# A 3x3 convolution in bf16: the first block's rows load ahead of the weights, and the fifth image pair loads in 8 and 56 rows

## The chip, the core and the metric

The kernel runs on one core of a Trainium2 chip. The metric is device time in microseconds of one execution. The core has five engines with an instruction stream each: TensorE (PE; its weight loads are listed as PEld), VectorE (DVE), ScalarE (ACT), GpSimd (POOL) and SyncE (SP). SyncE and GpSimd issue the DMAs of this kernel, each on a queue of its own (SyncE's is q1, GpSimd's q0), and 16 DMA engines carry them out.

## The reference

A 3x3 convolution with zero padding of 1, over 16 images of 64 channels of 64x64, to 128 output channels. The weights are 90% zeros, which the kernel does not use.

```python
batch, c_in, h, w, c_out, k = 16, 64, 64, 64, 128, 3
x_pad = np.pad(x, ((0, 0), (0, 0), (pad, pad), (pad, pad)))
output[b, co] += weight[co, ci, kh, kw] * x_pad[b, ci, kh:kh+h, kw:kw+w]   # over ci, kh, kw
```

In memory that is 16.8 MB of input, 0.3 MB of weights and 33.6 MB of output, all float32.

## The kernel before, in words

**Tiling.** The 16 images form 8 pairs: the 64 channels of two images fill the 128 partitions. Each pair's 64 rows are 4 blocks of 16 output rows, so there are 32 blocks, `k` from 0 to 31. A block is computed two rows at a time, in the manner of a fast convolution along the rows: with input rows a, b, c, d (a the odd row above, b and c the pair itself, d below), TensorE makes three products per block:

- `ps[0]`: (b + c) times the middle kernel row, G1. The sums b + c are the tile `sums`, made by `fill_sums`.
- `ps[1]`: odd rows (a and c) times G0 and G21 = G2 - G1. The odd rows are the tile `odd`, made by `fill_odd`.
- `ps[2]` or `ps[3]`: even rows (b and d) times G01 = G0 - G1 and G2. The even rows are the tile `even`, made by `fill_even`.

That is 6, 12 and 12 matmuls, 30 per block, half of them for each of the two images. ScalarE copies `ps[0]` to `pc` (L276); VectorE adds `pc` to `ps[1]` and to the last product and writes the even and odd output rows (L289, L293).

**Loads.** Pairs are loaded in bf16 by GpSimd's casting DMAs (`load`, L101 to 103), in the pieces that `PIECES` gives. Only the first 32 rows of pair 0 (`HEAD`) come in float32 by SyncE, into `x_head` (L98), behind the weights (L95). GpSimd issues the rest of pair 0 and pairs 1 to 3 at once; the pieces of pairs 4 to 7 are issued behind the blocks that `WHEN` names (L44, L269): pair 4's first piece behind block 1's fills, its second behind block 6's, and so on. Pair 4 comes in rows 0 to 28 and 28 to 64 (L41).

**Weights.** VectorE and ScalarE cast the 128x576 weights to bf16 in six pieces (L198). TensorE transposes them, three matmuls for each kernel row (L241), ScalarE copies G1 and G2 out of PSUM (L228, L230), VectorE copies G0 (L215) and makes the two differences G21 and G01 (L212). TensorE runs matmuls on a tile of zeros, `keep_busy`, ahead of the transposes and behind them, seven and seven (L237).

**Fills of block 0.** VectorE makes the sums between its two differences and the even rows behind them; ScalarE makes the odd rows behind its last weight copy. From block 1 on, GpSimd makes sums and even rows and ScalarE the odd rows, always one block or more ahead.

**Order of TensorE.** It waits for all four of ScalarE's weight steps, sets `s_free` to 1 itself, and enters a loop over two blocks at a time. In each block it takes `s_odd` and `s_sum`, makes the first product, takes `s_free`, makes the second, takes `s_even`, and makes the third.

**Stores.** SyncE stores a pair's 4.2 MB when its four blocks are done (L306), the last two pairs in halves, and the last half behind the section (L355). The four output buffers are used in turn; the fourth one, `home`, lies over `x_head` and the inputs of pairs 0 to 2.

Of the kernel before, what the change touches and what calls it, by code (L numbers as in the profile page):

```python
# [13 lines left out]
G0, G1, G2, G21, G01 = range(5)  # L14
# [8 lines left out]
def kernel(  # L23
# [6 lines left out]
    nc = tc.nc  # L30
    B, C_IN, H, W = x.shape
    C_OUT, _, KH, KW = weight.shape
    assert (B, C_IN, H, W) == (16, 64, 64, 64) and (C_OUT, KH, KW) == (128, 3, 3)
    NP = B // 2
    HEAD = 32
    N = NP * BLOCKS
    HALVED = (6, 7)

    PIECES = {p: [(0, H)] for p in range(NP)}
    PIECES[0] = [(HEAD, H)]  # L40
    PIECES[4] = [(0, 28), (28, H)]  # L41
    for p in (5, 6, 7):
        PIECES[p] = [(0, H // 2), (H // 2, H)]
    WHEN = {1: (4, 0), 6: (4, 1), 8: (5, 0), 11: (5, 1), 14: (6, 0), 17: (6, 1), 20: (7, 0), 24: (7, 1)}  # L44
# [4 lines left out]
    def sem(name):  # L49
        return nc.alloc_semaphore(name)  # L50

    def pair(p):
        return x[2 * p : 2 * p + 2].rearrange("n i h w -> (n i) h w")
# [4 lines left out]
    x_head = home[:, 0, :].rearrange("c (h w) -> c h w", w=W)  # L58
# [18 lines left out]
    pc = [sbuf(f"pc{k}", [128, 2, HALF, W], FP32) for k in range(3)]  # L77
    ps = [nc.alloc_psum_tensor(f"ps{k}", [128, 2, HALF, W], FP32).ap() for k in range(4)]

    s_w, s_head = sem("s_w"), sem("s_head")  # L80
    s_x = [[sem(f"s_x{p}{i}") for i in range(len(PIECES[p]))] for p in range(NP)]
    s_st = [[sem(f"s_st{p}{h}") for h in range(2 if p in HALVED else 1)] for p in range(NP)]
    s_dve, s_act, s_id, s_tr = sem("s_dve"), sem("s_act"), sem("s_id"), sem("s_tr")
    s_sum, s_even = ([sem(f"s_{n}{k}") for k in range(UNROLL)] for n in ("sum", "even"))
    s_odd, s_free = sem("s_odd"), sem("s_free")
    s_pe, s_pc, s_out, s_late = sem("s_pe"), sem("s_pc"), sem("s_out"), sem("s_late")

    def into(p, a, b):
        return out[2 * p : 2 * p + 2].rearrange("n o h w -> o n h w")[:, :, a:b, :]
# [2 lines left out]
    section.__enter__()  # L92


    nc.sync.dma_start(out=w_sb, in_=weight.rearrange("o i kh kw -> o (i kh kw)")).then_inc(  # L95
        s_w, 16
    )
    nc.sync.dma_start(out=x_head, in_=pair(0)[:, 0:HEAD, :]).then_inc(s_head, 16)  # L98


    def load(p, i=0):  # L101
        a, b = PIECES[p][i]
        nc.gpsimd.dma_start(out=xs[p][:, a:b, :], in_=pair(p)[:, a:b, :]).then_inc(s_x[p][i], 16)  # L103
# [5 lines left out]
        out=ident,  # L109
        in_=ident,  # L110
# [8 lines left out]
    def source(p, r):  # L119
        if r < 0 or r >= H:  # L120
            return None, None
        if p == 0 and r < HEAD:
            return x_head, (s_head, 16)
        return xs[p], (next(s for (a, b), s in zip(PIECES[p], s_x[p]) if r < b), 16)

    def rows_of(k, first, count):

        p = k // BLOCKS
        pieces = []
        for i, r in enumerate(range(first, first + 2 * count, 2)):  # L130
            src, landed = source(p, r)
            if pieces and pieces[-1][2] is src:
                pieces[-1][1] += 1
                pieces[-1][4].append(landed)
            else:
                pieces.append([i, 1, src, r, [landed]])
        return sorted(pieces, key=lambda q: q[2] is not None)
# [3 lines left out]
    def wait(engine, s, value):  # L141
        key = (engine.engine, s.name)
        if waited.get(key, 0) < value:
            engine.wait_ge(s, value)  # L144
            waited[key] = value

    def fill(engine, copy, zero, tile_, k, first, count, done):
        for i, c, src, r, landed in rows_of(k, first, count):
            if src is None:
                last = zero(tile_[:, i, :])  # L150
            else:
                for s in landed:
                    wait(engine, *s)
                last = copy(tile_[:, i : i + c, :], src[:, r : r + 2 * c - 1 : 2, :])
        last.then_inc(done, 1)

    def fill_odd(k, engine=None, copy=None, zero=None, done=None):
        r0 = ROWS * (k % BLOCKS)
        fill(
            engine or nc.scalar,  # L160
            copy or (lambda o, i: nc.scalar.copy(out=o, in_=i)),  # L161
            zero or (lambda o: nc.scalar.copy(out=o, in_=zeros)),
            odd[k % UNROLL], k, r0 - 1, HALF + 1, done or s_odd,
        )

    def fill_even(k, engine=None, copy=None, zero=None, done=None):
        r0 = ROWS * (k % BLOCKS)
        fill(
            engine or nc.gpsimd,
            copy or (lambda o, i: nc.gpsimd.tensor_copy(out=o, in_=i)),  # L170
            zero or (lambda o: nc.gpsimd.memset(o, 0.0)),  # L171
            even[k % UNROLL], k, r0, HALF + 1, done or s_even[k % UNROLL],
        )

    def fill_sums(k, engine=nc.gpsimd):
        p, b = divmod(k, BLOCKS)
        r0 = ROWS * b
        src = source(p, r0)[0]
        for r in (r0, r0 + ROWS - 1):
            wait(engine, *source(p, r)[1])  # L180
        engine.tensor_tensor(  # L181
            out=sums[k % UNROLL],
            in0=src[:, r0 : r0 + ROWS : 2, :],
            in1=src[:, r0 + 1 : r0 + ROWS : 2, :],
            op=ADD,
        ).then_inc(s_sum[k % UNROLL], 1)
# [6 lines left out]
    wps = {g: v.rearrange("o (j c) -> o j c", c=128) for g, v in  # L193
           ((G1, flat[2][:, 0, :]), (G0, flat[2][:, 1, :]), (G2, flat[3][:, 1, :]))}

    def cast(g, copy, a, b, done):
        k = 3 * g + a % 3
        copy(out=w_bf4[:, g, a:b, :], in_=w_v[:, k : k + b - a, :]).then_inc(done, 1)  # L198


    v = nc.vector
    v.memset(idle_rhs, 0.0).then_inc(s_dve, 1)  # L202
    v.wait_ge(s_w, 16)
    cast(G1, v.tensor_copy, 0, 3, s_dve)
    cast(G0, v.tensor_copy, 0, 3, s_dve)
    cast(G0, v.tensor_copy, 3, 4, s_dve)
    cast(G2, v.tensor_copy, 3, 4, s_dve)
    vcopy = lambda o, i: v.tensor_copy(out=o, in_=i)
    vzero = lambda o: v.memset(o, 0.0)

    def difference(g, wps):
        return v.tensor_tensor(out=wT[:, g], in0=wps[:, 0:3, :], in1=wT[:, G1], op=SUB)  # L212

    v.wait_ge(s_tr, 2)
    v.tensor_copy(out=wT[:, G0], in_=wps[G0][:, 0:3, :])  # L215
    v.wait_ge(s_act, 4)
    difference(G21, wps[G2])
    fill_sums(0, v)
    difference(G01, wps[G0])
    fill_even(0, v, vcopy, vzero)  # L220


    a = nc.scalar
    a.wait_ge(s_w, 16)
    cast(G1, a.copy, 3, 4, s_act)
    cast(G2, a.copy, 0, 3, s_act)
# [6 lines left out]
    t = nc.tensor  # L233

    def keep_busy(n):
        for _ in range(n):
            t.matmul(idle_ps, idle_rhs[:, 0:128], idle_rhs, start=True, stop=True)  # L237

    def transposed(g):
        for j in range(3):  # L240
            mm = t.matmul(  # L241
                wps[g][:, j, :], w_bf[:, g, C_IN * j : C_IN * (j + 2)], ident,
                start=True, stop=True,
            )
        mm.then_inc(s_tr, 1)

    t.wait_ge(s_dve, 1)
    keep_busy(7)
    t.wait_ge(s_id, 2)
    t.wait_ge(s_act, 1)  # L250
    t.wait_ge(s_dve, 2)
# [3 lines left out]
    t.wait_ge(s_dve, 5)  # L255
    t.wait_ge(s_act, 2)
    transposed(G2)
    keep_busy(7)


    g = nc.gpsimd
    for p in (1, 2, 3):
        load(p)
    for k in range(1, N):
        for fill_in, product in ((fill_sums, 2), (fill_even, 6)):
            if k >= UNROLL:
                wait(g, s_pe, 6 * (k - UNROLL) + product)
            fill_in(k)
        if k in WHEN:  # L269
            load(*WHEN[k])  # L270


    fill_odd(0)
    for k in range(N):
        wait(a, s_pe, 6 * k + 2)
        a.copy(out=pc[k % 3], in_=ps[0]).then_inc(s_pc, 1)  # L276
# [4 lines left out]
    for k in range(N):  # L281
        p, b = divmod(k, BLOCKS)
        o = outs[p % 4]
        r0 = ROWS * b
        if p >= 4:
# [4 lines left out]
            out=o[:, :, r0 : r0 + ROWS : 2, :], in0=ps[1], in1=pc[k % 3], op=ADD  # L290
# [3 lines left out]
            out=o[:, :, r0 + 1 : r0 + ROWS : 2, :], in0=ps[2 + k % 2], in1=pc[k % 3], op=ADD  # L294
# [4 lines left out]
    for p in range(NP):  # L299
        parts = 2 if p in HALVED else 1  # L300
        rows = H // parts
        for h in range(parts):
            if (p, h) == (NP - 1, 1):
# [3 lines left out]
                out=into(p, rows * h, rows * (h + 1)),  # L307
                in_=outs[p % 4][:, :, rows * h : rows * (h + 1), :],
# [22 lines left out]
    def take(s):  # L331
        t.wait_ge(s, 1).then_inc(s, -1)  # L332

    t.wait_ge(s_act, 4)
    t.sem_inc(s_free, 1)
    turn = t.alloc_register("turn")
    t.reg_mov(turn, 0)
    nc.br("blocks", engines=[PE])
# [15 lines left out]
    with tc.manual_schedule():  # L354
        nc.sync.dma_start(  # L355
            out=into(NP - 1, H // 2, H), in_=outs[(NP - 1) % 4][:, :, H // 2 : H, :]
# [36 lines left out]
```

## Time and profile before

| | |
|---|---|
| runs | 126.42 us, median of 3 (125.88 to 127.98) |
| profiled execution | 126.62 us, of which the span of its instructions is 124.8 us |
| busy share of the span | PE 88%, DVE 66%, POOL 52%, PEld 45%, ACT 44% |
| mean granted TensorE clock over the span | 0.963 (1.00 in every stretch until 115 us) |
| share of the DMA engines' time | q1 (SyncE) 66.9%, q0 (GpSimd) 31.0% |
| memory traffic | 17.07 MB read, 33.55 MB written, 406 GB/s over the span |
| SyncE's issues | weights 0.95, head 1.40, first store 22.73, last store 113.76 us |
| landing behind the issue | weights 2.8, head 5.9, pair 0's other half 8.0, pair 4's two pieces 17.1 and 13.4, last store 10.2 us |
| TensorE's first and last block | from 8.28, to 110.92 us |

A profile lists instructions by the line that issued them and by the tile that they write and read. Idle time of an engine is shown with what ended it. All times run from the first instruction of the span. The GB/s of a casting load count the bytes that it writes, in bf16; it reads twice as many.

### The profile page before, as it was taken

What the parts mean: (1) busy time and instruction counts of PE and PEld (TensorE: products, weight loads), DVE (VectorE), ACT (ScalarE), POOL (GpSimd) and SP (SyncE); (2) the same over time, 40 slices, a digit from 0 to 9 for tenths busy, and PEclk for the clock granted to TensorE, in tenths of its full rate; (3) what the DMA queues carried; (4) which work ended last, traced back from release to release, by engine and by line L of the source; (5) the groups of instructions that cost most, each with busy time, mean ns of one, the idle gap of its engine ahead of it and who ended that gap; (6) DMA issues with size and microseconds to landing.
All of it is one profiled execution on the core that took longest, in us unless ns stands there. A gap on an engine that the chain in (4) does not pass through costs nothing.

```text
span 124.8 us, 2486 instructions
## 1 busy us (share of the span) xinstructions
PE 110.0 (88%) x983; PEld 56.5 (45%) x983; DVE 82.6 (66%) x74; ACT 54.5 (44%) x78; POOL 64.3 (52%) x89
## 2 busy tenths in 40 slices
PE   5979999999999999999999999999999999990000
PEld 1435555555555555555555555555555555540000
DVE  0576777777777777777777777777777777773000
ACT  4524555555555555554444444444444555530000
POOL 4469555575755755755675575557555555100000
PEclk9999999999999999999999999999999999999555
DMA  3999999999999999999999999999999999999990
GB/s 109 350 219 221 215 218 213 191 429 407 342 330 285 390 410 356 338 427 349 374 370 345 364 432 345 341 416 420 352 339 428 431 407 428 423 428 428 426 391 32
DMA packets 4739, 42.79 MB, mean 343 GB/s; under 512 B 384, under 2 KB 384, under 8 KB 1664
## 3 DMA queue, kind: packets, MB, share of 16 engines
q1 hardware_dynamic: 3008, 34.90, 66.9%
q0 software_dynamic: 1728, 7.87, 31.0%
q14 instruction: 3, 0.02, 0.0%
HBM read 17.07 MB, written 33.55 MB: 406 GB/s over the span
## 4 chain that ended last, share of the span: by engine, by line
PE 82%; DVE 2%; issue 0%; DVEq 0%
PE ps L321 82%; DVE home L293 1%; DVE home L289 1%; DVEq L144 0%
## 5 line engine op out<-in xcount | busy, mean ns | idle before, releaser
L276 ACT COPY pc<-ps 128x1024 f32<-128x1024 f32 x32 | 32.4, 1012 | 51.9 <-PE ps L321 51.9
L321 PE MATMUL ps<-odd,wT 64*128 64x504 bf16 (+1 forms) x384 | 47.2, 377 | 0.0
L321 PE MATMUL ps<-even,wT 64*128 64x504 bf16 (+1 forms) x384 | 47.2, 377 | 0.0
L289 DVE TENSOR_TENSOR o<-ps,pc 128x1024 f32<-128x1024 f32 x24 | 29.4, 1225 | 19.6 <-PE ps L321 19.6
L321 PEld LDWEIGHTS ps<-even,wT 64*128 64x128 bf16 x384 | 21.6, 94 | 19.9
L321 PEld LDWEIGHTS ps<-odd,wT 64*128 64x128 bf16 x384 | 21.6, 94 | 19.9
L293 DVE TENSOR_TENSOR o<-ps,pc 128x1024 f32<-128x1024 f32 x24 | 29.4, 1225 | 0.0
L321 PE MATMUL ps<-sums,wT 64*128 64x504 bf16 (+1 forms) x192 | 26.5, 377 | 0.7 <-PEq L332 0.7
L181 POOL TENSOR_TENSOR sums<-x 128x512 bf16<-128x512 bf16 x20 | 23.1, 1154 | 0.1
L170 POOL COPY even<-x 128x576 bf16<-128x576 bf16 (+1 forms) x20 | 13.0, 650 | 19.2 <-PE ps L321 19.2
L321 PEld LDWEIGHTS ps<-sums,wT 64*128 64x128 bf16 x192 | 10.7, 94 | 10.9 <-issue 1.2
L181 POOL TENSOR_TENSOR sums<-home 128x512 bf16<-128x512 bf16 (+1 forms) x11 | 13.3, 1212 | 2.8 <-DMA home<-in_x_dram 2.8
L289 DVE TENSOR_TENSOR home<-ps,pc 128x1024 f32<-128x1024 f32 x8 | 9.8, 1225 | 6.3 <-PE ps L321 6.3
L161 ACT COPY odd<-x 128x576 bf16<-128x576 bf16 (+1 forms) x20 | 13.2, 660 | 0.0
L170 POOL COPY even<-home 128x576 bf16<-128x576 bf16 (+2 forms) x11 | 6.7, 609 | 8.2 <-PE ps L321 8.0
L293 DVE TENSOR_TENSOR home<-ps,pc 128x1024 f32<-128x1024 f32 x8 | 9.8, 1225 | 0.0
L161 ACT COPY odd<-home 128x576 bf16<-128x576 bf16 (+1 forms) x10 | 6.6, 657 | 0.0
L171 POOL MEMSET even<- 128x64 bf16 x8 | 1.2, 151 | 10.3 <-PE ps L321 10.3
L237 PE MATMUL ps<-idle_rhs 128*128 128x512 bf16 x14 | 5.3, 538 | 1.4 <-DVE idle_rhs L202 1.4
L103 POOL DMA_DIRECT2D x<-in_x_dram x9 | 5.1, 565 | 0.0
L237 PEld LDWEIGHTS ps<-idle_rhs 128*128 128x128 bf16 x14 | 1.7, 129 | 3.7 <-issue 1.9
L198 DVE CAST w_bf<-w_sb 128x192 bf16<-128x192 f32 (+1 forms) x4 | 1.1, 352 | 2.4 <-DMA w_sb<-in_weight_dram 2.4
(21 smaller groups left out, 15.2 us busy)
## 6 DMA issues: line engine op xcount, KB each, us to landing
out_dram<-o SPq DMA_DIRECT2D x5, 4096.0 KB, 18.4
out_dram<-home SPq DMA_DIRECT2D x1, 4096.0 KB, 19.1
out_dram<-o SPq DMA_DIRECT2D x2, 2048.0 KB, 14.4
out_dram<-home SPq DMA_DIRECT2D x2, 2048.0 KB, 11.1
x<-in_x_dram POOLq DMA_DIRECT2D x6, 512.0 KB, 13.1
home<-in_x_dram POOLq DMA_DIRECT2D x2, 1024.0 KB, 13.5
home<-in_x_dram SPq DMA_DIRECT2D x1, 1024.0 KB, 5.9
x<-in_x_dram POOLq DMA_DIRECT2D x1, 1024.0 KB, 20.0
```

Of the source, the lines that this page charges most:

```text
L103: nc.gpsimd.dma_start(out=xs[p][:, a:b, :], in_=pair(p)[:, a:b, :]).then_inc(s_x[p][i], 16)
L161: copy or (lambda o, i: nc.scalar.copy(out=o, in_=i)),
L170: copy or (lambda o, i: nc.gpsimd.tensor_copy(out=o, in_=i)),
L171: zero or (lambda o: nc.gpsimd.memset(o, 0.0)),
L181: engine.tensor_tensor(out=sums[k % UNROLL], in0=src[:, r0 : r0 + ROWS : 2, :], in1=src[:, r0 + 1 : r0 + ROWS : 2, :], op=ADD,).then_inc(s ...
L198: copy(out=w_bf4[:, g, a:b, :], in_=w_v[:, k : k + b - a, :]).then_inc(done, 1)
L237: t.matmul(idle_ps, idle_rhs[:, 0:128], idle_rhs, start=True, stop=True)
L276: a.copy(out=pc[k % 3], in_=ps[0]).then_inc(s_pc, 1)
L289: v.tensor_tensor(out=o[:, :, r0 : r0 + ROWS : 2, :], in0=ps[1], in1=pc[k % 3], op=ADD).then_inc(s_free, 1)
L293: v.tensor_tensor(out=o[:, :, r0 + 1 : r0 + ROWS : 2, :], in0=ps[2 + k % 2], in1=pc[k % 3], op=ADD).then_inc(s_out, 1)
L321: mm = t.matmul(into[:, n, :, c_lo:c_hi], tap(g, kw, n), src[q, i : i + HALF, c_lo + kw - 1 : c_hi + kw - 1], start=(m == 0), stop=(m == l ...
```

## The change

The head load is cut in two: 17 rows ahead of the weights, 15 behind them, with a semaphore each. Block 0 needs input rows 0 to 16 alone. Its three fills now stand ahead of the weights' steps: the sums first on VectorE, the odd rows first on ScalarE (behind the clear of the zeros tile), the even rows on GpSimd (behind its loads) instead of VectorE. TensorE waits for three of ScalarE's steps instead of four; VectorE releases the second product with its first difference (`s_free`), and the third with its second difference, for which it waits until GpSimd's even rows are done (`s_first`). The fillers are nine ahead of the transposes and three behind them, instead of seven and seven. Pair 4 is loaded as rows 0 to 8 and 8 to 64; the times at which its two pieces are issued stay.

```diff
-    HEAD = 32
+    HEAD, FIRST = 32, 17
...
-    PIECES[4] = [(0, 28), (28, H)]
+    PIECES[4] = [(0, 8), (8, H)]
...
-    s_w, s_head = sem("s_w"), sem("s_head")
+    s_w, s_head = sem("s_w"), [sem(f"s_head{i}") for i in range(2)]
...
-    s_odd, s_free = sem("s_odd"), sem("s_free")
+    s_odd, s_free, s_first = sem("s_odd"), sem("s_free"), sem("s_first")
...
+    def load_head(i, a, b):
+        nc.sync.dma_start(out=x_head[:, a:b, :], in_=pair(0)[:, a:b, :]).then_inc(s_head[i], 16)
+
+    load_head(0, 0, FIRST)
     nc.sync.dma_start(out=w_sb, in_=weight.rearrange("o i kh kw -> o (i kh kw)")).then_inc(
         s_w, 16
     )
-    nc.sync.dma_start(out=x_head, in_=pair(0)[:, 0:HEAD, :]).then_inc(s_head, 16)
+    load_head(1, FIRST, HEAD)
...
         if p == 0 and r < HEAD:
-            return x_head, (s_head, 16)
+            return x_head, (s_head[0 if r < FIRST else 1], 16)
...
     v.memset(idle_rhs, 0.0).then_inc(s_dve, 1)
+    fill_sums(0, v)
     v.wait_ge(s_w, 16)
...
     v.wait_ge(s_act, 4)
-    difference(G21, wps[G2])
-    fill_sums(0, v)
-    difference(G01, wps[G0])
-    fill_even(0, v, vcopy, vzero)
+    difference(G21, wps[G2]).then_inc(s_free, 1)
+    v.wait_ge(s_first, 1)
+    difference(G01, wps[G0]).then_inc(s_even[0], 1)
...
     a = nc.scalar
+    a.wait_ge(s_dve, 1)
+    fill_odd(0)
     a.wait_ge(s_w, 16)
...
-    keep_busy(7)
+    keep_busy(9)
...
     transposed(G2)
-    keep_busy(7)
+    keep_busy(3)
...
     for p in (1, 2, 3):
         load(p)
+    fill_even(0, done=s_first)
...
-    fill_odd(0)
     for k in range(N):
         wait(a, s_pe, 6 * k + 2)
...
-    t.wait_ge(s_act, 4)
-    t.sem_inc(s_free, 1)
+    t.wait_ge(s_act, 3)
```

More of the change, by code (lines that the diff above doesn't have):

```diff
@@ L207 @@
     cast(G2, v.tensor_copy, 3, 4, s_dve)
-    vcopy = lambda o, i: v.tensor_copy(out=o, in_=i)
-    vzero = lambda o: v.memset(o, 0.0)
     def difference(g, wps):
```

## Prediction

> **What bounds the kernel now.** I read the page first, then the chain of waits that ended last, then stretches of the span with their DMA share, then the timeline of SyncE's issues, and last the timeline of the first ten microseconds, where the change sits. The page's head, its DMA slices and its HBM line:
>
> ```profile
> span 124.8 us, 2486 instructions
> ...
> DMA  3999999999999999999999999999999999999990
> ...
> HBM read 17.07 MB, written 33.55 MB: 406 GB/s over the span
> ```
>
> The chain that ended last:
>
> ```profile
> 8.28 102.64 PE ps L321 x948
> ...
> 112.24 1.23 DVE home L293
> ```
>
> The two seem to disagree. The chain says: TensorE runs from 8.28 us without a hole to 110.92, VectorE finishes, and whatever starts TensorE sooner ends the kernel sooner. The DMA row says that the 16 DMA engines are full from the second slice to the last but one. The stretches decide (columns: stretch, its length, busy time of PE, PEld, DVE, ACT, POOL, the granted TensorE clock, DMA share, GB/s moved):
>
> ```profile
> 1.00:2.00 1.00, 0.60 (x2) 0.28 (x3) 0.27 (x1) 1.00 (x1) 0.55 (x1) 1.00 0.05 12
> 2.00:3.00 1.00, 1.00 (x4) 0.30 (x2) 0.00 (x0) 0.19 (x1) 0.65 (x3) 1.00 0.97 261
> 3.00:8.00 5.00, 4.54 (x20) 1.88 (x18) 2.90 (x8) 2.46 (x6) 2.20 (x4) 1.00 1.04 307
> 8.00:22.00 14.00, 13.72 (x128) 7.23 (x130) 10.28 (x11) 6.51 (x10) 9.56 (x13) 1.00 1.05 218
> ...
> 24.00:25.00 1.00, 1.00 (x13) 0.53 (x10) 1.00 (x2) 0.00 (x0) 0.26 (x1) 1.00 1.01 176
> 25.00:26.00 1.00, 1.00 (x13) 0.48 (x11) 0.94 (x1) 0.64 (x1) 0.98 (x3) 1.00 1.24 456
> ...
> 97.00:101.00 4.00, 4.00 (x41) 2.04 (x37) 2.71 (x3) 2.43 (x5) 2.57 (x3) 1.00 1.02 438
> 105.00:113.80 8.80, 7.19 (x68) 3.49 (x62) 6.88 (x6) 2.60 (x3) 0.70 (x2) 1.00 1.01 428
> 113.80:121.00 7.20, 0.00 (x0) 0.00 (x0) 0.00 (x0) 0.00 (x0) 0.00 (x0) 0.62 1.01 428
> 121.00:122.00 1.00, 0.00 (x0) 0.00 (x0) 0.00 (x0) 0.00 (x0) 0.00 (x0) 0.50 0.45 188
> 122.00:123.00 1.00, 0.00 (x0) 0.00 (x0) 0.00 (x0) 0.00 (x0) 0.00 (x0) 0.50 0.12 49
> ```
>
> From 2.0 us to 121 us the DMA share is about 1.0 in every stretch: loads alone until 25, loads and stores mixed, stores alone at 428. (A casting load counts its bf16 bytes, so 218 is 436 read.) The end confirms it. After 113.8 us the queues still move 7.2 us at 428 GB/s plus about 0.24 MB, 3.3 MB in all, while the last store, issued at 113.76, holds 2.1 MB. So 1.2 MB, 2.8 us of work, lay ahead of it. **The kernel is bound by the DMA engines, not by TensorE**: 17.07 MB read and 33.55 MB written pass in 119 us, and TensorE has slack at its end. The last row also shows that some engines finish up to 2 us after most: the span ends with the slowest of the 16.
>
> **What the change touches, from the timeline of the start:**
>
> ```profile
> 3.74 1.15 DVE L198 CAST w_bf<-w_sb 128x192 bf16<-128x192 f32 x4 [2.40 <-DMA w_sb<-in_weight_dram]
> ...
> 5.44 2.10 PE L237 MATMUL ps<-idle_rhs 128*128 128x512 bf16 x7
> ...
> 7.37 0.69 DVE L181 TENSOR_TENSOR sums<-home 128x512 bf16<-128x512 f32 x1 [0.62 <-DMA home<-in_x_dram]
> ...
> 8.28 0.82 PE L321 MATMUL ps<-sums,wT 64*128 64x512 bf16 x6 [0.74 <-PEq L332]
> ```
>
> Today the weights are seen at 3.74; the 32 head rows at 7.37, and the sums that VectorE makes from them let block 0 go at 8.28.
>
> **Head split, 17 rows ahead of the weights.** SyncE issues three DMAs instead of two (0.39 and 0.42 us each, from 0.95): 0.95, 1.40, 1.82. First bytes come at 2.0, as now, and a request issued at 1.82 is in time for a queue that is full beyond 4, so no hole opens. The 17 rows are 17 x 256 B x 128 = 557 KB; at the 350 to 390 GB/s seen between 3 and 6 us that is 1.5 us (1.3 at 428, 1.8 at the 307 of 3 to 8). The rows are seen at about 4.1 (2.0 + 1.5, and the 0.6 that the weights' landing shows behind their last bytes), the weights at 3.74 + 1.5 = 5.24 instead of 3.74. The last 15 rows land with the same bytes before them as the 32 did, 7.4 plus nothing I can see. The price of cutting a transfer: rows of 16 KB go at 438 GB/s (97 to 101 us), rows of 8 KB at 428 (105 to 113.8), so halving a row costs at most 2.3%, 0.06 us on 1.05 MB.
>
> **Work moved into the wait for the weights.** Sums (0.692 us, VectorE) run at 4.1 to 4.8, odd rows (0.247 + 0.617 us, ScalarE; the zero row right behind the table load, which ends at 2.19) end at 4.75, both before 5.24. Even rows go from VectorE (0.741) to GpSimd (0.603 for 128x512, so some 0.68 for 128x576): GpSimd has issued its loads by 4.66, so 4.7 to 5.4, inside its 2.77 us wait, ahead of the sums of block 1, which wait for the last 15 rows (7.42 now). All of it costs nothing while the weights are the later of the two. If the 17 rows came after the weights' turn instead, ScalarE's 0.62 would stand ahead of its weight casts and the chain below would slip by up to 0.6.
>
> **Weights to block 0.** Today's transposes run from 4.38 and the filler behind them from 5.44, 1.70 after the weights are seen. Three fillers instead of seven are 3 x 0.30 = 0.90 us. So block 0 can go at 5.24 + 1.70 + 0.90 = 7.84, or 8.1 if the last transpose's modelled end (5.64) counts: **8.0, 0.3 us earlier** than 8.28 (7.7 to 8.6 with the ends of the head's rate). The wait on TensorE is now for three of ScalarE's steps, not four; the first difference releases the odd product: 6.75 - 3.74 = 3.0 behind the weights, 8.25, and that product is due at 8.0 + 0.64 = 8.64. The second follows at 8.8, due at 9.94; behind it on VectorE waits only the first output sum, due at 10.2. Without these margins of 0.4 and 1.1 us TensorE would wait for VectorE. The seven-to-nine fillers ahead of the weights fill a longer wait.
>
> **Fifth pair in 8 and 56 rows.** Queued before the first store there are now 20 rows fewer: 655 KB read, 1.5 us at 436. The load queue, which hands over to stores at 25.0, runs out at 23.5. The first store is issued 14.45 us behind block 0's start (22.73 - 8.28): 22.45 now. The SyncE request of 0.95 moves bytes from 2.0, so a store into an empty queue starts about 1.05 behind its issue: 23.5. The hand-over is just closed, 0 expected. The 56 rows, issued at about 25.1, carry 655 KB more and land later: the 36 rows land at 25.35 + 13.4 = 38.8 now, 3 us more at half the engines is 41.8. GpSimd first needs them for block 16's sums at 54.6. A row of 1 KB after the cast may be slow: the weights' 2.3 KB rows ran at 261 GB/s in their second, so 262 KB cost between 0.6 and 1.0 us; I take +0.1 of that 0.4.
>
> The Trainium skill, page "DMA: Bandwidth & Descriptors", section "Anatomy of one DMA", speaks against cutting transfers: each DMA has a fixed cost of about 2.0 us beside bytes over 436 GB/s. By it the one DMA more could make the sum 126.5 + 2.0 = 128.5. The trace sides with hiding: the stretch 105 to 113.8 holds the join between two stores and shows a share of 1.01.
>
> **The sum**, against the profiled execution's own 126.62 us (span 124.8, 1.8 outside it): bytes unchanged, first byte unchanged, +0.06 for the head, +0.1 for the short rows, 0 for the hand-over (0 to +0.6 if block 0 goes at 8.6), 0 for TensorE's 0.3 since it has slack. 126.8. That execution lies 0.2 above the median of the three runs, so for the median: 126.42 + 0.15, **126.5 us**.
>
> **Rivals.**
> *The end follows TensorE* (chance 0.13). The chain says so. Then the gain is what block 0 gains, 0.3, at most 0.6: 126.1. Against: 1.2 MB queued ahead of the last store. A gain of 2% is out of reach even so: block 0 would have to start at 5.8, 0.5 us after the weights are there.
> *The weights come late, and the load-to-store hand-over opens* (0.10, slower). If the weights were served with all of the head, they would be seen at 7.4, block 0 would go at 7.4 + 2.75 = 10.2, the first store at 24.6, its bytes at 25.7, against loads that end at 23.5: 2.2 us of empty engines. It decides from a block 0 later than 8.0, one for one. The engines that finish early have up to 2 us to give; the last one reads some 1.5 us longer, so between 0.5 and 2.2 is paid: 127.9. For: loads from GpSimd are in the queues as well. Against: SyncE's head, issued at 1.40, landed in 5.9 us and GpSimd's half pair, issued at 1.45, in 8.0, so what SyncE asks is not held up by it; and the weights are issued ahead of the rest.
> A rule of the Trainium skill, same page, section "Queues, rings and completion order", that engines go round robin between queues, would support this rival; the two landings do not show it here at the start.
> *A bubble per DMA* (0.05). One more request with a hole of its own: the weights' 288 KB took 2.8 us to land, 2.1 more than 0.7 of transfer: 128.6. The Trainium skill's fixed cost per DMA, cited above, would act like this.
> *The 56 rows are late* (0.02): only if they land 13 us later than worked out; a stall of 3 us would give 129.5.
>
> **How the numbers follow.** Forecast 0.70: 126.5, own range 126.0 to 127.2, as runs of the kernel before lie at 125.88 to 127.98 and the slowest engine moves the end by some tenths. The range 125.6 to 127.8 takes in the first rival and most of the second. A measurement here can tell about 2% (2.5 us) from no change. Faster by that has no mechanism but an evener finish of the DMA engines (2 us at most): 0.03. Slower: the late rows, and the upper ends of hand-over and bubble: 0.07. Within: 0.90.
>
> **What would show it.** In the changed kernel's profile: weights seen near 5.2, sums near 4.1, block 0 near 8.0, DMA share 1.0 in every stretch from 2 to 121 and no dip between 23 and 26, the last store landing about 10.5 us behind its issue (10.2 now, plus what TensorE gained). A wrong forecast would show as a stretch with a share under 0.9 before 121, or an end that moves with block 0.

## The result, and the profile after

The changed kernel takes 129.09 us (median of 6 runs, 128.90 to 129.23) against 125.99 for the kernel before (125.75 to 127.98): a ratio of 1.0244, 95% interval 1.0223 to 1.0266 (the ratio leaves out the one slow execution, 127.98). It is **slower by 3.1 us**; the forecast was 126.5, and the range ended at 127.8. The profiled execution took 129.23 us, span 127.4, which is 2.6 more than the span before; the profile before is of an execution of 126.62, 0.6 above its median, so the profiles differ by less than the medians. The page's head, DMA row and HBM line:

```profile
span 127.4 us, 2482 instructions
...
DMA  3999999699999999999999999999999999999991
...
HBM read 17.07 MB, written 33.55 MB: 397 GB/s over the span
```

The bytes are the same. The DMA row now has a 6 in its eighth slice, near 24 us, where it had a 9. The stretches of the changed kernel (columns as before: stretch, length, PE, PEld, DVE, ACT, POOL, clock, DMA share, GB/s):

```profile
2.00:4.00 2.00, 2.00 (x7) 0.67 (x5) 0.00 (x0) 0.43 (x2) 1.62 (x5) 1.00 0.83 228
...
8.00:10.00 2.00, 2.00 (x10) 0.53 (x9) 1.46 (x3) 0.48 (x1) 0.00 (x0) 0.58 1.14 288
10.00:12.00 2.00, 2.00 (x14) 0.75 (x12) 0.00 (x0) 1.14 (x2) 0.08 (x1) 0.57 1.01 218
...
24.00:25.00 1.00, 1.00 (x14) 0.46 (x10) 0.65 (x1) 0.93 (x2) 1.00 (x2) 1.00 0.39 62
25.00:25.60 0.60, 0.60 (x10) 0.24 (x8) 0.16 (x1) 0.60 (x2) 0.27 (x1) 1.00 0.07 27
...
26.00:30.00 4.00, 4.00 (x40) 1.84 (x38) 3.20 (x4) 1.58 (x2) 2.40 (x4) 1.00 1.00 418
...
115.70:124.00 8.30, 0.00 (x0) 0.00 (x0) 0.00 (x0) 0.00 (x0) 0.00 (x0) 0.61 1.01 426
```

Three things are new: a slow start (228 GB/s from 2 to 4 us), a TensorE clock of 0.57 to 0.58 from 8 to 12 us, and DMA engines that are more than half empty from 24 to 25 and nearly empty from 25 to 25.6 (shares of 0.39 and 0.07). The end is as before: after the last store's issue the engines are full at 426. The start, for comparison, in the kernel before:

```profile
2.00:4.00 2.00, 2.00 (x7) 0.60 (x4) 0.26 (x1) 0.45 (x3) 1.62 (x5) 1.00 1.08 326
```

The timeline of the changed kernel (start, duration, engine, line), in two excerpts, the second of TensorE and SyncE alone:

```profile
1.87 0.42 SPq L96 DMA_DIRECT2D home<-in_x_dram  x1
...
5.50 0.69 DVE L185 TENSOR_TENSOR sums<-home 128x512 bf16<-128x512 f32 x1 [4.15 <-DMA home<-in_x_dram]
...
6.41 1.15 DVE L202 CAST w_bf<-w_sb 128x192 bf16<-128x192 f32 x4 [0.23 <-DMA w_sb<-in_weight_dram]
...
7.05 0.95 PE L245 MATMUL ps<-ident,w_bf 128*128 128x128 bf16 x9 [1.83 <-DVE w_bf L202]
...
11.92 1.27 POOL L185 TENSOR_TENSOR sums<-home 128x512 bf16<-128x512 f32 x1 [5.21 <-DMA home<-in_x_dram]
```

```profile
8.79 1.46 PE L325 MATMUL ps<-sums,wT 64*128 64x512 bf16 x6
...
13.47 0.81 PE L325 MATMUL ps<-sums,wT 64*128 64x512 bf16 x6
```

```profile
24.68 26.31 SPq L310 DMA_DIRECT2D out_dram<-o  x3
```

The 17 rows are seen at 5.50 (4.1 was forecast), the weights at 6.41 (5.24), block 0 goes at 8.79 (8.0). The last 15 rows, issued at 1.87, are seen only at 11.92 (7.4 was forecast): GpSimd waits 5.2 us for them. Block 1 starts 4.7 us behind block 0 instead of 3.24 (13.47 behind 8.79; in the kernel before 11.52, below, behind 8.28), and the first store is issued at 24.68 instead of 22.73.

```profile
11.52 0.83 PE L321 MATMUL ps<-sums,wT 64*128 64x512 bf16 x6
```

**Why the last 15 rows are late.** The DMA queues from 7 to 10 us, the kernel before first, then the changed one (packets, MB, share of 16 engines):

```profile
q0 software_dynamic: 129, 0.66, 107.1%
q1 hardware_dynamic: 1, 0.00, 0.0%
```

```profile
q0 software_dynamic: 102, 0.49, 78.8%
q1 hardware_dynamic: 99, 0.36, 31.2%
```

Before, SyncE's 32 rows shared the engines with GpSimd's loads from 4 to 7 us (98 packets of q1, 63 of q0) and were through at 7. Now SyncE has a third request behind the other two, and its 15 rows (q1) still share the engines with the loads from 7 to 10, packet by packet: 99 packets against 102. The Trainium skill, page "DMA: Bandwidth & Descriptors", section "Queues, rings and completion order", says that an engine goes round robin between its queues; this trace agrees (99 against 102), and the 15 rows of 3.8 KB were paired with loads that read 8 and 16 KB. Part of the lateness is the slow start: in e9 below, where the loads come a little later, the rows are seen at 9.9, still not at 7.4.

**Where the rest of the time went.** From 30 to 34 us, first before, then after:

```profile
q1 hardware_dynamic: 73, 1.20, 71.3%
q0 software_dynamic: 62, 0.29, 34.9%
```

```profile
q1 hardware_dynamic: 73, 1.20, 93.8%
q0 software_dynamic: 12, 0.09, 10.3%
```

The same 73 store packets took 71.3% of the engines' 4 us in one kernel and 93.8% in the other: 0.62 and 0.82 us each. The share is full both times, the bytes are not: with the loads counted by what they read (twice their MB) 1.20 + 0.58 = 1.78 MB before, 1.38 MB after. **A full DMA share is not a full rate.** The stretch lies just ahead of where the load queue, which ran dry at 25, comes back with the 56 rows: the first of them move at 33, and from 31 to 33 the stores, alone in the engines, took 1.0 us each (110.0% of 32 us, 16 engines times 2 us, over 35 packets):

```profile
q1 hardware_dynamic: 35, 0.57, 110.0%
```

Against the kernel before, the changed one lost in bytes, at the 428 GB/s of the end: 0.20 MB from 2 to 4 us (0.5 us), 0.47 MB from 24 to 26 (0.85 against 0.38; 1.1 us), 0.40 MB from 30 to 34 (0.9 us). That is 2.5 us; smaller stretches bring it to 2.9 by 42 us (table below), against 2.6 us more of span, so the account closes to some 0.3 us.

### The profile page after: what moved, and what is told of

Same layout as the page of the kernel before. It is cut to its first block, busy times and chain, and to the rows that moved or that the text cites. A ratio compares the mean times of both kernels' runs of the same rounds, so it can differ in the third digit from the quotient of the medians.

```text
span 127.4 us, 2482 instructions
## 1 busy us (share of the span) xinstructions
PE 110.8 (87%) x981; PEld 48.7 (38%) x981; DVE 82.0 (64%) x73; ACT 54.8 (43%) x78; POOL 64.8 (51%) x90
## 4 chain that ended last, share of the span: by engine, by line
PE 83%; DMA 4%; DVE 3%; SPq 0%; issue 0%; DVEq 0%
PE ps L325 82%; DMA w_sb<-in_weight_dram 4%; DVE home L297 1%; DVE home L293 1%; DVE w_bf L202 1%; PE ps L241 1%; PE ps L245 0%; SPq L96 0%; SPq L391 0%; DVEq L148 0%; SPq L92 0%
## 5 line engine op out<-in xcount | busy, mean ns | idle before, releaser
L325 PE MATMUL ps<-even,wT 64*128 64x504 bf16 (+1 forms) x384 | 46.7, 377 | 0.0
L325 PEld LDWEIGHTS ps<-odd,wT 64*128 64x128 bf16 x384 | 18.9, 96 | 23.8 <-issue 1.6
L325 PEld LDWEIGHTS ps<-even,wT 64*128 64x128 bf16 x384 | 18.6, 94 | 22.9
L325 PEld LDWEIGHTS ps<-sums,wT 64*128 64x128 bf16 x192 | 9.3, 95 | 12.0 <-issue 1.1
L241 PE MATMUL ps<-idle_rhs 128*128 128x512 bf16 x12 | 4.8, 569 | 1.4 <-DVE idle_rhs L206 1.4
L185 DVE TENSOR_TENSOR sums<-home 128x512 bf16<-128x512 f32 x1 | 0.7, 691 | 4.2 <-DMA home<-in_x_dram 4.2
L165 ACT CAST odd<-home 128x512 bf16<-128x512 f32 (+2 forms) x3 | 1.5, 512 | 3.6 <-DMA home<-in_x_dram 3.6
## 6 DMA issues: line engine op xcount, KB each, us to landing
x<-in_x_dram POOLq DMA_DIRECT2D x1, 896.0 KB, 14.5
```

The source lines that it names most:

```text
L185: engine.tensor_tensor(out=sums[k % UNROLL], in0=src[:, r0 : r0 + ROWS : 2, :], in1=src[:, r0 + 1 : r0 + ROWS : 2, :], op=ADD,).then_inc(s ...
L325: mm = t.matmul(into[:, n, :, c_lo:c_hi], tap(g, kw, n), src[q, i : i + HALF, c_lo + kw - 1 : c_hi + kw - 1], start=(m == 0), stop=(m == l ...
```

## The experiments

For all kernels the table gives what the profiled execution shows: when block 0 starts, when the first store is issued, the MB moved between 2 and 42 us (q1 plus twice q0, of the DMA view of that stretch), how far that falls short of the kernel before, in us at 428 GB/s, and by how much that same execution is above 125.95 us, the median of the kernel before; then the median and the ratio of the timed comparison.

| kernel | block 0 | first store | MB, 2 to 42 | short, us | above, us | median us | ratio (95%) |
|---|---|---|---|---|---|---|---|
| before | 8.28 | 22.73 | 16.70 | | | 125.9 to 126.0 | |
| changed | 8.79 | 24.68 | 15.44 | 2.9 | 3.3 | 129.09 | 1.022 to 1.027 |
| e1_cushion_back | 9.25 | 24.69 | 15.75 | 2.2 | 1.9 | 128.32 | 1.017 to 1.021 |
| e2_short_piece_alone | 8.45 | 22.89 | 16.18 | 1.2 | 1.8 | 126.68 | 1.004 to 1.007 |
| e3_late_tensor | 9.34 | 23.80 | 16.06 | 1.5 | 1.3 | 127.63 | 1.011 to 1.016 |
| e4_three_pieces | 8.74 | 24.54 | 15.20 | 3.5 | 3.7 | 129.80 | 1.027 to 1.039 |
| e5_loads_two_blocks_earlier | 8.46 | 24.61 | 16.49 | 0.5 | 0.4 | 126.34 | 1.002 to 1.005 |
| e6_late_tensor_early_loads | 9.76 | 24.22 | 16.47 | 0.5 | 0.6 | 126.56 | 1.001 to 1.009 |
| e7_clock_kept | 8.55 | 24.46 | 15.46 | 2.9 | 3.5 | 129.49 | 1.025 to 1.037 |
| e8_before_early_loads | 7.95 | 22.40 | 16.47 | 0.5 | 0.6 | 126.56 | 1.004 to 1.008 |
| e9_start_mended | 8.48 | 22.95 | 16.16 | 1.3 | 1.5 | 128.17 | 1.017 to 1.021 |
| e10_second_piece_later | 8.11 | 22.56 | 16.39 | 0.7 | 0.7 | 126.65 | 1.004 to 1.008 |
| e11_changed_early_loads | 9.45 | 24.73 | 16.52 | 0.4 | 0.9 | 126.38 | 0.998 to 1.006 |
| e12_start_mended_28 | 8.52 | 23.00 | 16.44 | 0.6 | 0.8 | 126.85 | 1.005 to 1.010 |

The two columns in us go together within 0.6: but for near neighbours, what the queues moved by 42 us orders the kernels. (Their zeros differ: the 16.70 MB are of the execution of 126.62 us, 0.7 above 125.95.) From 42 to 115 us every kernel is within 0.1 MB of the kernel before, so what is short at 42 is still to be moved at the end. The column of the first store does not: 24.2 to 24.7 stands beside 126.3 as well as beside 129.8.

**Is it the DMA engines or TensorE?** The first four runs undo or add one thing each.

```diff
# e1: the changed kernel, and
-    PIECES[4] = [(0, 8), (8, H)]
+    PIECES[4] = [(0, 28), (28, H)]
```

> The changed kernel with pair 4 again in rows 0 to 28 and 28 to 64; the head split, the moved fills and the fillers stay as changed. Theory 1 (the DMA engines bound the kernel, and the change starved them between loads and the first store): TensorE stays as late as in the changed kernel (first store issued near 24.7), but the loads now last until about 25.5, so the stretch 24 to 26 has a DMA share near 1.0 and the kernel returns to 126.0 plus the 0.6 that the start still loses: 126.3 to 126.9. Rival (the end follows TensorE): TensorE is as late as in the changed kernel, so the time stays at 128.5 to 129.1.

128.32. Neither number, though near the rival's. The hole at 24 to 26 was gone (0.36 MB on q0 and 0.18 on q1, 0.90 MB read and written), but from 30 to 34 it moved 1.41 MB and from 36 to 42 1.98 (2.44 before).

```diff
# e2: the kernel before, and
-    PIECES[4] = [(0, 28), (28, H)]
+    PIECES[4] = [(0, 8), (8, H)]
```

> The kernel before with one edit: pair 4 in rows 0 to 8 and 8 to 64. Theory 1: first store issued at 22.7, its bytes near 23.7, loads run out near 23.5 to 25: a hole of 0.2 us or less and a time of 125.9 to 126.5. Rival A (the 56 rows cost by themselves, the slow stores of 30 to 42 us in the changed kernel, 1.4 us of engine time): 127.2 to 127.6. Rival B (the end follows TensorE): TensorE starts as before, 126.0.

126.68: the pieces alone cost 0.7, with TensorE nearly where it was; between the forecasts. No hole at 24 to 26, 1.39 MB from 30 to 34. The profile is of the slowest of its six executions (127.73), so the size of that loss is not the median's.

```diff
# e3: the kernel before, and
     transposed(G2)
-    keep_busy(7)
+    keep_busy(17)
```

> The kernel before with ten more fillers behind the transposes (17 instead of 7), so that block 0 starts about 1.4 us later, at 9.7, and everything on TensorE with it; pieces as before. Theory 1: the first store is issued near 24.1, its bytes near 25.1, when the loads are just ending: no hole, 125.9 to 126.5. Rival (the end follows TensorE): 126.0 + 1.4 = 127.4.

127.63: the rival's number. But TensorE was only 1.1 us late (9.34 against 8.28; 1.4 was planned), and the time rose by 1.7. My theory 1, that lateness is free as long as the engines stay full, fell in this form. The trace showed no hole, but 1.45 MB from 30 to 34 us instead of 1.78, and 2.09 MB from 36 to 42 instead of 2.44, where the first store's packets end and the second's begin.

```diff
# e4: the changed kernel, and
-    PIECES[4] = [(0, 8), (8, H)]
+    PIECES[4] = [(0, 8), (8, 36), (36, H)]
-    WHEN = {1: (4, 0), 6: (4, 1), 8: (5, 0), ...
+    WHEN = {1: (4, 0), 6: (4, 1), 7: (4, 2), 8: (5, 0), ...
```

> The changed kernel with pair 4 in three pieces, rows 0 to 8, 8 to 36 and 36 to 64, the third issued behind block 7. The hole between loads and stores stays as in the changed kernel. If the slow stores of 30 to 42 us come from the long rows of the 56-row piece, they go and the time falls by 1.0 to 1.4, to 127.7 to 128.1. If they come from the engines having started the stores all at once behind the hole, they stay: 128.8 to 129.3.

129.80, worse than both forecasts: without the long rows of the 56-row piece the loss stayed, so they are not what makes it. 30 to 34 improved a little (1.43 MB), 36 to 42 fell to 1.89.

The theory that was left: the DMA engines bound the kernel, but they keep their rate only while neither queue has run dry and has to come back. (In this plain form it is too strong, as e10 and e12 show below.) Then TensorE's lateness should cost nothing once the loads are issued earlier.

```diff
# e5: e1, and
-    WHEN = {1: (4, 0), 6: (4, 1), 8: (5, 0), 11: (5, 1), 14: (6, 0), 17: (6, 1), 20: (7, 0), 24: (7, 1)}
+    WHEN = {1: (4, 0), 4: (4, 1), 6: (5, 0), 9: (5, 1), 12: (6, 0), 15: (6, 1), 18: (7, 0), 22: (7, 1)}
# e6: e3, and the same; e8: the kernel before, and the same; e11: the changed kernel, and the same
```

> The changed kernel with pair 4 again in rows 0 to 28 and 28 to 64, and every load from pair 4's second piece on issued two blocks earlier (behind blocks 4, 6, 9, 12, 15, 18 and 22). TensorE stays late: block 0 near 8.8 to 9.3, first store issued near 24.7, as in the run with the 28 rows alone (128.3). Theory 1 in the form that the first four runs leave (the DMA engines bound the kernel, and lose time wherever one of the two queues runs dry and starts again while the other runs: 31 to 34 us and 38 to 42 us): GpSimd's queue no longer runs dry before 40 us, both slow stretches shrink, and the time falls to 126.4 to 127.3 with TensorE as late as before. Rival (the end follows TensorE, which is 2 us late): it stays at 128.0 to 128.5.

126.34: 2.0 us less than e1 by the load schedule alone. The first store's issue, and the queues from 30 to 34 us, of e5:

```profile
24.61 0.40 SPq L310 DMA_DIRECT2D out_dram<-o  x1
```

```profile
q1 hardware_dynamic: 83, 1.36, 80.2%
q0 software_dynamic: 50, 0.18, 21.9%
```

The store is as late as in the changed kernel, and its packets are back at 80.2% of 64 us over 83, 0.62 us each. The stretch moves 1.72 MB.

> The kernel before with ten more fillers (block 0 about 1.1 us later, as in the run of 127.6) and with every load from pair 4's second piece on issued two blocks earlier. Theory 1: 125.9 to 126.5, the late TensorE costs nothing once the load queue does not run dry. Rival (the end follows TensorE): 127.3 to 127.8.

> The kernel before with every load from pair 4's second piece on issued two blocks earlier, and nothing else: what the earlier loads do by themselves. Theory 1: the queues did not run dry in the kernel before, so 125.7 to 126.1, no change. Rival: if the stores that start later behind the longer load queue push the end, 126.5 to 127.5.

Both took 126.56. That e8 is slower than the kernel before was the rival's number and not what I expected. It moved 0.29 MB less from 24 to 30 us (2.23 against 2.52), most of it from 24 to 26, when load packets ran alone, 0.38 us each (112.1% of 32 us over 95), and the store issued at 22.40 had not begun. But e6 against e8 is the cleanest test of lateness. Block 0 and the last store's issue of e6, then of e8:

```profile
9.76 0.82 PE L321 MATMUL ps<-sums,wT 64*128 64x512 bf16 x6
...
115.26 0.37 SPq L355 DMA_DIRECT2D out_dram<-home  x1
```

```profile
7.95 0.83 PE L321 MATMUL ps<-sums,wT 64*128 64x512 bf16 x6 [0.94 <-PEq L332]
...
113.43 0.37 SPq L355 DMA_DIRECT2D out_dram<-home  x1
```

1.8 us apart on TensorE in the profiled executions, from block 0 to the last store, and the same median: the spans end 9.5 us behind the last store's issue in e6 and 11.3 in e8. The rival, that the end follows TensorE, is out.

> The changed kernel, 8 and 56 rows as they are, with every load from the 56 rows on issued two blocks earlier. TensorE is as late as in the changed kernel, the first store issued near 24.6. Theory 1: the 56 rows are behind the 8 in the queue before it runs dry, no hole at 24 to 26, no slow stretch at 30 to 34 and 38 to 42: 126.3 to 127.0, although the pieces and the start are those of the changed kernel. Rival (the pieces or TensorE's lateness cost by themselves): 128.0 to 129.1.

126.38, not to be told from the kernel before. Pieces of 8 and 56 rows, the split head and a late TensorE are all there; only the loads behind the 8 rows were issued earlier.

> The kernel before with one edit: pair 4's second piece is issued behind block 7 instead of block 6, 3.3 us later (28.7). Stores fill the engines meanwhile, and TensorE is not touched. If GpSimd's queue having run dry costs when it starts again (the slow stores of 30 to 34 us), the time rises by 0.5 to 0.9, to 126.4 to 126.9. If full engines are all that counts, 125.9 to 126.1.

```diff
# e10: the kernel before, and
-    WHEN = {1: (4, 0), 6: (4, 1), 8: (5, 0), ...
+    WHEN = {1: (4, 0), 7: (4, 1), 8: (5, 0), ...
```

126.65, with TensorE untouched: 0.7 for one load issued one block later. The size was as expected, the place was not. The load queue was dry from 26 to 33 us, as in the changed kernel, and came back at no price: the stores beside it from 33 to 34 took 0.62 us each, and from 30 to 34 it moved 1.69 MB, near the 1.78 before. The loss is at 36 to 42. First before, then e10:

```profile
q0 software_dynamic: 168, 0.64, 53.6%
q1 hardware_dynamic: 87, 1.16, 48.0%
```

```profile
q0 software_dynamic: 193, 0.77, 75.8%
q1 hardware_dynamic: 54, 0.64, 25.7%
```

The first store, for a while without loads beside it, ends sooner, and the store queue is the one that has to come back: 2.18 MB instead of 2.44, and the load packets took 0.38 us each instead of 0.31.

**Why is the first store late?** Two suspects: the halved clock, and the last 15 head rows.

```diff
# e7: the changed kernel, and
-    keep_busy(9)
+    keep_busy(16)
```

> The changed kernel with 16 fillers instead of 9 ahead of the transposes, so that TensorE has no 1.8 us hole ahead of them. If the halved clock of 8 to 12 us is what makes the first store late, it is issued near 23.3 and the time falls to about 127.7. If the last 15 head rows (seen at 11.9, so that block 1's sums end at 13.2) hold block 1 anyway, the clock stays at 1.0 but block 1 still starts near 13.2 to 13.3, the first store comes at 24.4 to 24.5 and the time falls by no more than 0.3, to 128.8.

129.49: nothing gained (the second alternative, whose signs in the trace all came, had 128.8). The clock stayed at 1.00 from 8 to 12 us. TensorE and GpSimd of e7:

```profile
10.52 1.48 PE L325 MATMUL ps<-even,wT 64*128 64x512 bf16 x12
13.26 0.83 PE L325 MATMUL ps<-sums,wT 64*128 64x512 bf16 x6 [1.26 <-PEq L336]
```

```profile
11.84 1.27 POOL L185 TENSOR_TENSOR sums<-home 128x512 bf16<-128x512 f32 x1 [4.93 <-DMA home<-in_x_dram]
```

At full clock block 0 ends sooner, and then TensorE waits 1.26 us for block 1's sums, which GpSimd can begin only at 11.84, when the 15 rows are there, and has at 13.1. The slow clock had been hidden behind these rows; the first store is issued at 24.46.

```diff
# e9: e7, and GpSimd's first load behind the identity; e12: e9 with pair 4 in 28 and 36 rows
-    load(0)
     nc.gpsimd.memset(ident, 0.0).then_inc(s_id, 1)
     ...
     ).then_inc(s_id, 1)
+    load(0)
```

> The changed kernel with 16 fillers ahead of the transposes and GpSimd's first load issued behind the two steps that make the identity (some 1.5 us later), so that the last 15 head rows do not share the engines with it; pieces of 8 and 56 rows stay. The 15 rows are seen at 7 to 8 instead of 11.9, block 1 starts about 3.3 us behind block 0, the first store is issued near 23.0 instead of 24.7. Theory 1: no hole left at 24 to 26; what stays is the start's 0.4 to 0.5 and the slow restart of GpSimd's queue near 30 to 34 that the kernel before with 8 and 56 rows paid (0.7): 126.9 to 127.4. Rival (the short first piece is what costs, whenever the store comes): 128.5 to 129.1.

> As the run with the start mended, and pair 4 again in 28 and 36 rows: head split, moved fills and fillers stay. First store near 23.0. Theory 1: only the start's 0.4 to 0.5 of DMA time is left over the kernel before: 126.2 to 126.6. Rival (TensorE's end decides): block 0 is 0.3 later than in the kernel before, 126.3; the two cannot be told apart here, but both say that nothing else of the change costs.

In e9 the load was issued only 0.44 us later (1.89; the identity moved forward instead), and the 15 rows were seen at 9.9 (7 to 8 was expected), but block 1 came on time:

```profile
9.92 1.27 POOL L185 TENSOR_TENSOR sums<-home 128x512 bf16<-128x512 f32 x1 [3.07 <-DMA home<-in_x_dram]
...
11.74 0.83 PE L325 MATMUL ps<-sums,wT 64*128 64x512 bf16 x6
```

The first store went out at 22.95 and the hole was gone (0.92 MB from 24 to 26); 30 to 34 stayed low (1.44 MB). The profiled execution took 127.42, but the median is 128.17, 0.8 above the forecast. Two of the other three executions had spans as short (125.2 and 125.3 us against 125.4), and what they took longer lies outside the span, 2.9 and 3.2 us against 2.0; why is in no trace, and stays open. e12, with 28 rows, took 126.85, 0.25 above its forecast: without hole and without slow stretches (its 24 to 42 us moved 7.69 MB, more than the 7.57 before) the start's loss is what is left, 0.38 MB of the 2 to 24 us. Here too the load queue ran dry, from 28 to 30 us, and came back at full rate, with the stores at 0.62 us each (82.7% of 32 us over 43). The kernel before did the same, first the queues from 27 to 29, then from 29 to 31:

```profile
q1 hardware_dynamic: 55, 0.90, 105.2%
```

```profile
q1 hardware_dynamic: 41, 0.67, 79.6%
q0 software_dynamic: 14, 0.06, 15.8%
```

So a queue that has run dry does not always cost on its way back. What is shown is narrower: in the four kernels with the loads two blocks earlier (e5, e6, e8, e11) the stretch from 30 to 34 us moved 1.67 to 1.72 MB and 36 to 42 moved 2.51 to 2.59.

No version beat the kernel before.

## Why the prediction was wrong

**What held.** The DMA engines bound the kernel, not TensorE: e6 against e8, e5 against e1, and e11 show it. The rival "the end follows TensorE" had chance 0.13 and is excluded. "A bubble per DMA" named 128.6, near what came, but e12 and e11 issue the same three requests and took 126.85 and 126.38, so a price of 2.1 us per request is not there. (The section of the Trainium skill quoted for that rival describes GpSimd's path; the request added here is SyncE's.) The 56 rows were not late for block 16: issued at 27.3, they landed 14.5 us later, at 41.8, with block 16 some 14 us off. The moves of sums, odd and even rows cost nothing, as worked out, because the weights came later still.

**The step that failed first** is "The last 15 rows land with the same bytes before them as the 32 did, 7.4 plus nothing I can see". They were seen at 11.92. I had read from two landings (5.9 and 8.0 us) that what SyncE asks is not held up by GpSimd's loads. But a landing does not show who shared the engines: from 4 to 7 us the queues of the kernel before already ran side by side, 98 packets against 63. The round-robin rule that I quoted and set aside was the right one, not for the weights but for the rows behind them. The late rows set the time of block 1, which my sum never followed: I had followed block 0 alone, and "14.45 us behind block 0's start" for the first store became 15.9.

**Mis-sized.** The 17 rows at 350 to 390 GB/s: the stretch of 2 to 4 us ran at 228, so they were seen 1.4 us later than forecast, the weights 1.2. (The prediction's own row for 2 to 3 us, the first bytes of the kernel before, had 261.) Block 0 came 0.8 us later than forecast, and 0.5 us of DMA time went, against +0.06 in the sum. The filler step left a hole of 1.83 us ahead of the transposes; its price was hidden (e7).

**The hand-over**, "just closed, 0 expected", opened: 0.47 MB, 1.1 us, because the store was issued at 24.68 and not at 22.45. The rival that described it had the first store at 24.6 (24.68 came) and decided from a block 0 later than 8.0; its route was another one, and its price of 127.9 counted the hole alone. Its chance of 0.10 was low for a step that I had worked out to be just closed, without slack.

**What was in no term:** the slow stretches behind the hand-over. I took a DMA share of 1.0 for a full rate, and the bytes as all that can cost. From 30 to 34 us the share was full and the bytes 22% fewer. So a late store cost more than its hole, and e3 cost 1.7 with no hole at all.

Not shown: why packets stretch around the time when the other queue comes back, and why they sometimes do not. The traces show where it happens (16 KB stores of 0.62 us at 0.82 on average, load packets of 0.31 us at 0.38) and where it does not (the kernel before, e10 and e12 when their load queue came back). Loads that were issued two blocks earlier avoided it from 30 to 42 us. e10 and e4 moved the loss from one stretch to the next without predicting which, and e8 shows that earlier is not better everywhere: it lost 0.6 us, most of it in the 2 us before its first store began.

## What to carry to other kernels

Where the DMA engines bound a kernel, read MB per stretch, with casting loads counted by what they read, and not the busy share; here a queue that ran dry often, not always, cost on its way back as well as while it was empty. When a transfer is moved behind another one, look at which other queue will be running beside it by then, and follow every consumer of what is moved, here block 1 and not only block 0. A step that comes out just balanced can fall either way: give its failure a chance to match, and keep slack there.

## What the hardware showed beyond that

TensorE's granted clock fell to 0.58 from 8 to 12 us although it had been idle for only 1.83 us (5.22 to 7.05), with nine matmuls and three fillers behind the gap; with the gap filled (e7) it stayed at 1.00. Four more runs had a gap there of 1.55 to 2.17 us (e5, e4, e1, e11), and their clock from 8 to 10 us was 0.50 to 0.66; with a gap of 0.57 (e9) it was 1.00. The Trainium skill, page "TensorE: Matmul & The Clock Gate", section "Part 1: The HAM clock gate", gives an idle window of about 3.4 us for that; in this trace a shorter gap came ahead of the drop.

A store issued into empty engines began to move 0.9 us later (24.68 to 25.6), close to the 1.05 that the first request showed (0.95 to 2.0).
